# A decoder trunk in split fp32: column units split while token tile 1's first steps are issued

## The chip, the cores and the metric

The kernel runs on one core of one Trainium2 chip. The metric is the device time of one execution in microseconds (us), as the median of several runs; lower is better.

## The reference, cut to what matters

Two layers; each is a feed-forward sub-layer (FFN), a token-mixing sub-layer (Mix) and a second FFN, so six sub-layers one behind the other. All products are over 256 tokens and a model width of 1024.

```python
for l in range(DEPTH):                       # DEPTH = 2
    h = rms_norm(x, ffn1_pre_g[l])
    x = x + 0.5 * rms_norm(swiglu(h, ffn1_w1[l], ffn1_w2[l]), ffn1_post_g[l])
    h = rms_norm(x, mix_pre_g[l])
    z = h @ w_in[l]
    q, k, v, u_s, v_s, g_a, g_b = jnp.split(z, IN_SPLIT_POINTS, axis=-1)
    y_attn = sliding_window_attention(q, k, v, attn_sinks[l])
    y_sgu = spatial_gating(gelu(u_s), gelu(v_s), sgu_ln_g[l], sgu_ln_b[l], sgu_w[l], sgu_b[l])
    merged = (sigmoid(g_a) * (y_attn @ w_attn_branch[l])
              + sigmoid(g_b) * (y_sgu @ w_sgu_branch[l]))
    x = x + rms_norm(merged @ w_out[l], mix_post_g[l])
    h = rms_norm(x, ffn2_pre_g[l])
    x = x + 0.5 * rms_norm(swiglu(h, ffn2_w1[l], ffn2_w2[l]), ffn2_post_g[l])
```

## The kernel before, in words

**Split products.** Every fp32 operand is held as two parts, a high part (rounded) and a low part (what the rounding left), and a product is three matmuls: high by high, high by low, low by high (`passes`, and `feature_major` at L259 to L261, whose third matmul reads the low part of the weights).

**Weight units.** The weights come in units of 128x1024 floats (512 KB). `Stream` handles them in one fixed order. A unit is loaded by a DMA that SyncE issues (L119) into one of 4 `raw` buffers; ScalarE casts it to the high part (`wh`, L138); VectorE subtracts to get the low part (`wl`, L152, in `low`). Only then is the raw buffer free, so `low` of unit u issues the load of unit u + 4. The split pair goes into a ring of 9 places. `st.upto(n)` splits units in order up to n, and stops when the ring has no room (`free`); `st.done(u)` gives a place back. After the start, `slip` is set: the subtraction of a unit is issued behind the cast of the next, or where somebody calls `low`.

**Order.** The order of the instructions of every engine is the order in which the Python code calls them; nothing is moved by a scheduler, and each engine takes its own in that order.

**Between two sub-layers.** `project` multiplies the last product of a sub-layer, closes it (norm, residual, norm of the next one), and issues the next sub-layer's first product, whose rows are weight rows (`first`): token tile 0's `steps` first, then `finish(0, ...)`, then token tile 1's `steps`. A step is a few matmuls of one or half a unit. For tile 1 the first eight steps are `hi + lo` (four units of which are outside the ring), the others are `rest`. In `rest`, step 0 is preceded by `high` and `low` of tile 0 (L523 on ScalarE and L527 on VectorE: the input of the column products, scaled, in two parts), step `turn0` by a turn of tile 0's result, and behind every second step one unit of the column products is split (L597, L598). In Mix `turn0` is 2, and the turn is a transposition on TensorE (L380), a cast on ScalarE (L381), and on VectorE a chain of 16 instructions (L384 to L398) that normalises `vs`. A second such turn, that of tile 1, comes in `middle` ahead of column unit 4.

**Column products.** `middle` multiplies the column units. In Mix these are eight units u0 to u7 of `self.u`, then eight of `self.q`, and so on, each 24 matmuls of 256 columns (L259 to L261). Here u8 and on stand for the units behind u7, so u8 is the first of `self.q`. Behind unit j, `upto` splits as far as unit j + 7. Attention starts behind the fourteenth unit (L717, L718); it reads the queries that ScalarE and VectorE take out of PSUM (L841, L844). In an FFN the column units are taken by `feature_pair` (L272), 16 matmuls each.

Of the kernel before, what the change touches and what calls it, by code (L numbers as in the profile page):

```python
# [40 lines left out]
AHEAD = 7  # L41
# [22 lines left out]
def trunk(ctx: ExitStack, tc: tile.TileContext, a: dict, out: bass.AP):  # L64
# [100 lines left out]
    st = Stream()  # L165
# [237 lines left out]
    def project(units, lhs, k_post, gpost, gpre, nxt, xt, behind=None):  # L403
# [110 lines left out]
        first = nxt.first  # L514
# [4 lines left out]
        def quarter(t, h):  # L519
            return og[t].rearrange("p (a b) -> p a b", a=KD)[:, h * 4:h * 4 + 4, :]  # L520

        def high(t, h, ps):
            nc.scalar.copy(xth[:, h * 4:h * 4 + 4, rows_of(t)], ps)  # L523

        def low(t, h, ps):
            at = (slice(None), slice(h * 4, h * 4 + 4), rows_of(t))
            nc.vector.tensor_tensor(out=xtl[at], in0=ps, in1=f(xth[at]), op=ALU.subtract)  # L527
# [19 lines left out]
        hi, lo, rest = first.steps(0, xth, xtl)[:3]  # L547
# [36 lines left out]

        first.begin(1)
        hi, lo, rest = first.steps(1, xth, xtl)[:3]
        for s in hi + lo:
            s()
        for i, s in enumerate(rest):
            if i == 0:  # L590
                for h in range(2):
                    high(0, h, quarter(0, h))
                    low(0, h, quarter(0, h))
            if i == first.turn0:
                turn0()
            s()
            if i % 2:  # L597
                st.upto(min(st.ready + 1, first.units[-1] + 1 + AHEAD))  # L598
# [333 lines left out]
    first = subs[0].first  # L932
# [104 lines left out]
    for i, sub in enumerate(subs):  # L1037
        last = i == len(subs) - 1
        nxt = None if last else subs[i + 1]
        gains = []  # L1040

        def early():

            gains.append(gain(sub.post, i // 3))
            if not last:
                gains.append(gain(nxt.pre, (i + 1) // 3))
            if i == 0:
                nc.sync.dma_start(sinks, a["attn_sinks"].unsqueeze(0).partition_broadcast(P))
            if isinstance(nxt, Mix):
                nxt.tables()  # L1050

        behind = sub.middle(both, *xt, turn1, early)
        turn1 = project(sub.rows, sub.lhs, sub.k_post, gains[0], None if last else gains[1], nxt, xt, behind)
# [54 lines left out]
```

## Time and the profile before

| what | value |
|---|---|
| median of 3 runs | 1203.17 us (1202.26 to 1206.29) |
| the profiled execution: its time / its span | 1199.29 us / 1197.6 us |
| TensorE (PE) busy | 1176.7 us, 98% of the span |
| VectorE (DVE) / ScalarE (ACT) busy | 835.8 us (70%) / 677.9 us (57%) |
| mean granted TensorE clock | 0.996 |
| DMA | 220.90 MB, mean 184 GB/s |

The span runs from the first to the last instruction; the 1.7 us between it and the execution's own time lie around it. PE is the engine of the matmuls and PEld its weight loads; an engine's row names the source line, the operation, the tile it writes and the tile it reads. Idle time of an engine is put down to the instruction that ended it.

### The profile page before, as it was taken

Reading aid. Unit: us, or ns where it says so; the run is one execution under the profiler, and the core shown is the slowest. Engines: PE = TensorE matmul, PEld = TensorE weight load, DVE = VectorE, ACT = ScalarE, POOL = GpSimd, SP = SyncE. Lnnn points to the kernel's source line nnn. Section 1 sums busy time; section 2 is a strip of 40 time slices with the busy share of each in tenths; the row PEclk is TensorE's granted clock in tenths of the full one; section 3 lists DMA queues with packets and bytes.
Section 4 is the critical chain, followed back from the end, with each engine's and each line's share of the span. In section 5 each row is a group of like instructions: output and inputs, shape, how many; then the busy total and the mean of one; then the engine's idle time right before and its main releaser. Section 6 shows DMA issues by size and latency. Waiting matters only on the chain.

```text
span 1197.6 us, 18409 instructions
## 1 busy us (share of the span) xinstructions
PE 1176.7 (98%) x7031; PEld 1047.8 (87%) x7031; DVE 835.8 (70%) x1423; ACT 677.9 (57%) x1143; POOL 60.0 (5%) x40
## 2 busy tenths in 40 slices
PE   9999999999999999999999999999999999999997
PEld 7888888899999888888888888888999998888886
DVE  6767748678775976666576776577878768676653
ACT  5657544447676555655455665444567664665641
POOL 0000000001112100000000000000012040000000
PEclk9999999999999999999999999999999999999999
DMA  7577674465456637558626657735544664565660
GB/s 246 182 251 235 218 240 132 137 226 157 127 153 206 201 96 239 194 185 261 222 83 219 219 188 258 222 113 176 187 150 133 185 197 137 171 199 192 198 208 35
DMA packets 61288, 220.90 MB, mean 184 GB/s; under 512 B 7056, under 2 KB 7056, under 8 KB 61200
## 3 DMA queue, kind: packets, MB, share of 16 engines
q1 hardware_dynamic: 60912, 219.46, 56.3%
q8 instruction: 55, 0.90, 0.3%
q14 instruction: 33, 0.27, 0.1%
q10 hardware_dynamic: 288, 0.27, 0.1%
HBM read 218.65 MB, written 1.05 MB: 183 GB/s over the span
## 4 chain that ended last, share of the span: by engine, by line
PE 87%; DVE 6%; DMA 3%; ACT 1%; issue 1%; SPq 0%; DVEq 0%; ACTq 0%
PE mm L272 34%; PE mm L252 31%; PE mm L261 6%; PE mm L259 6%; PE mm L260 6%; DMA raw<-in_w_in 3%; DVE wl L152 2%; PE mm L217 1%; PE mm L754 1%; ACT wh L138 1%; DMA raw<-in_ffn_w 1%; PE mm L717 1%; PE mm L718 1%; PE mm L767 0%; PE mm L766 0%
## 5 line engine op out<-in xcount | busy, mean ns | idle before, releaser
L152 DVE TENSOR_TENSOR wl<-raw,wh 128x1024 fp32r<-128x1024 f32 x372 | 454.6, 1251 | 114.2 <-ACT wh L138 113.5
L138 ACT CAST wh<-raw 128x1024 fp32r<-128x1024 f32 x372 | 382.6, 1050 | 192.7 <-DMA raw<-in_ffn_w 75.1
L272 PE MATMUL mm<-xt,wh 128*128 128x512 f32 x1152 | 290.7, 393 | 0.7 <-DVE xt L948 0.7
L252 PE MATMUL mm<-wh,m 128*128 128x512 f32 x832 | 258.7, 390 | 0.0
L272 PEld LDWEIGHTS mm<-xt,wh 128*128 128x128 f32 x1152 | 207.6, 189 | 38.2 <-DVE xt L948 1.2
L252 PEld LDWEIGHTS mm<-wh,m 128*128 128x128 f32 x832 | 156.3, 188 | 32.0
L272 PEld LDWEIGHTS mm<-xt,wl 128*128 128x128 f32 x1152 | 157.2, 191 | 11.2
L252 PE MATMUL mm<-wl,m 128*128 128x512 f32 x416 | 162.1, 390 | 0.0
L272 PE MATMUL mm<-xt,wl 128*128 128x256 f32 x1152 | 160.7, 283 | 0.0
L261 PE MATMUL mm<-xt,wl 128*128 128x256 f32 x512 | 146.7, 287 | 5.0 <-DVE wl L152 5.0
L259 PE MATMUL mm<-xt,wh 128*128 128x256 f32 x512 | 147.7, 289 | 0.0
L260 PE MATMUL mm<-xt,wh 128*128 128x256 f32 x512 | 146.2, 285 | 0.0
L632 DVE TENSOR_TENSOR t<-mm,t 128x256 f32<-128x256 f32 x144 | 60.7, 422 | 96.8 <-ACT t L631 96.8
L261 PEld LDWEIGHTS mm<-xt,wl 128*128 128x128 f32 x512 | 99.5, 194 | 5.4 <-DVE wl L152 5.4
L260 PEld LDWEIGHTS mm<-xt,wh 128*128 128x128 f32 x512 | 99.6, 195 | 0.2
L259 PEld LDWEIGHTS mm<-xt,wh 128*128 128x128 f32 x512 | 99.6, 195 | 0.2
L252 PEld LDWEIGHTS mm<-wl,m 128*128 128x128 f32 x416 | 78.2, 188 | 15.9
L631 ACT COPY t<-mm 128x256 f32<-128x256 f32 x144 | 52.9, 367 | 46.5 <-PE mm L272 46.2
L634 ACT ACTIVATE t<-t 128x256 f32<-128x256 f32 x72 | 30.1, 418 | 75.9 <-DVE t L632 75.9
L259 PE MATMUL mm<-m,wh 128*128 128x256 f32 x256 | 72.7, 284 | 0.0
L260 PE MATMUL mm<-m,wh 128*128 128x256 f32 x256 | 72.5, 283 | 0.0
L261 PE MATMUL mm<-m,wl 128*128 128x256 f32 x256 | 72.5, 283 | 0.0
(156 smaller groups left out, 1327.3 us busy)
## 6 DMA issues: line engine op xcount, KB each, us to landing
raw<-in_ffn_w SPq DMA_DIRECT2D x264, 512.0 KB, 4.4
raw<-in_w_in SPq DMA_DIRECT2D x84, 512.0 KB, 4.4
raw<-in_w_sgu_branch SPq DMA_DIRECT2D x16, 512.0 KB, 3.7
raw<-in_w_attn_branch SPq DMA_DIRECT2D x16, 512.0 KB, 4.4
raw<-in_w_out SPq DMA_DIRECT2D x16, 512.0 KB, 4.6
gain<-in_ffn_post_g SPq DMA_DIRECT2D x4, 512.0 KB, 6.5
gain<-in_ffn_pre_g SPq DMA_DIRECT2D x3, 512.0 KB, 6.2
x<-in_x SPq DMA_DIRECT2D x4, 256.0 KB, 4.3
```

The source lines that it names most:

```text
L138: nc.scalar.copy(h, self.raw[u])
L152: nc.vector.tensor_tensor(out=lo, in0=self.raw.pop(u), in1=f(h), op=ALU.subtract)
L217: nc.tensor.transpose(ps[:, k, :], src[:, (c0 + k) * P:(c0 + k + 1) * P], ident)
L252: nc.tensor.matmul(o, every[i][0], every[i][1], start=start and i == 0, stop=stop and i == 2)
L259: nc.tensor.matmul(o, wh[:, ks], ah[:, k, :], start=(k == 0), stop=False)
L260: nc.tensor.matmul(o, wh[:, ks], al[:, k, :], start=False, stop=False)
L261: nc.tensor.matmul(o, wl[:, ks], ah[:, k, :], start=False, stop=(k == KD - 1))
L272: nc.tensor.matmul(out_, w[:, k * P:(k + 1) * P], x, start=(i == 0), stop=(i == len(todo) - 1))
L631: nc.scalar.copy(y[:, half, :], o[half][:, S:2 * S])
L632: nc.vector.tensor_tensor(out=y[:, half, :], in0=o[half][:, 0:S], in1=y[:, half, :], op=ALU.add)
L634: nc.scalar.activation(y[:, 0, :], y[:, 0, :], AF.Silu)
L717: nc.tensor.matmul(s[r][:, i, :], q_, kth[:, g, 0:nk], start=True, stop=False)
```

## The change

While token tile 1's eight first steps (`hi + lo`) are issued, one unit is split behind the first, third, fifth and seventh of them, if the ring has a place.

```diff
         first.begin(1)
         hi, lo, rest = first.steps(1, xth, xtl)[:3]
-        for s in hi + lo:
+        for i, s in enumerate(hi + lo):
             s()
+            if i % 2 == 0:
+                st.upto(min(st.ready + 1, first.units[-1] + 1 + AHEAD))
         for i, s in enumerate(rest):
             if i == 0:
                 for h in range(2):
```

`project` issues this between every two sub-layers, so five times. Of the ring's 9 places, 6 are held by the first units of a Mix at that point and 4 by those of an FFN, which leaves 3 and 5. The number of instructions of each kind stays as it was; only places in the queues change. In the rows below a tile's name ends in running numbers; raw_341_1820, raw_344_1826, raw_345_1829 and raw_403_2033 are the raw buffers of the units u0 to u3 of layer 0's Mix.

ScalarE, between FFN1 and Mix of layer 0, from the cast of tile 0's values (L373) on; before:

```order
L373 ACTIVATE vv_410_2105<-mm_404_2059,ry_398_2021 128x2x64
L523 CAST xt_74_352<-t4_348_1833 128x4x128 x2
L138 CAST wh_417_2160<-raw_341_1820 128x1024
L381 CAST kth_411_2106<-mm_419_2163 128x2x128
L138 CAST wh_431_2206<-raw_344_1826 128x1024
L138 CAST wh_435_2219<-raw_345_1829 128x1024
L138 CAST wh_438_2231<-raw_403_2033 128x1024
L138 CAST wh_441_2243<-raw_433_2210 128x1024
L138 CAST wh_444_2255<-raw_437_2223 128x1024
```

and now:

```order
L373 ACTIVATE vv_410_2105<-mm_404_2059,ry_398_2021 128x2x64
L138 CAST wh_417_2124<-raw_341_1820 128x1024
L138 CAST wh_419_2135<-raw_344_1826 128x1024
L138 CAST wh_422_2147<-raw_345_1829 128x1024
L523 CAST xt_74_352<-t4_348_1833 128x4x128 x2
L138 CAST wh_425_2175<-raw_403_2033 128x1024
L381 CAST kth_411_2106<-mm_428_2181 128x2x128
L138 CAST wh_440_2224<-raw_421_2139 128x1024
L138 CAST wh_444_2237<-raw_424_2151 128x1024
L138 CAST wh_447_2249<-raw_427_2179 128x1024
```

The casts of u0, u1 and u2 now stand ahead of the two L523, and four casts instead of one ahead of L381.

VectorE at the same place. Before, the subtractions of u0 to u4 stand behind the end of the turn's chain:

```order
L396 SCALAR_TENSOR_TENSOR n8_409_2104<-n8_409_2104,mv_421_2172,gain_412_2107 128x1024
L398 SCALAR_TENSOR_TENSOR n8_409_2104<-n8_409_2104,ry_430_2190,gain_413_2109 128x1024
L152 TENSOR_TENSOR wl_418_2161<-raw_341_1820,wh_417_2160 128x1024
L152 TENSOR_TENSOR wl_432_2207<-raw_344_1826,wh_431_2206 128x1024
L152 TENSOR_TENSOR wl_436_2220<-raw_345_1829,wh_435_2219 128x1024
L152 TENSOR_TENSOR wl_439_2232<-raw_403_2033,wh_438_2231 128x1024
L152 TENSOR_TENSOR wl_442_2244<-raw_433_2210,wh_441_2243 128x1024
```

Now three of them stand ahead of the chain's first instruction (L384):

```order
L374 SCALAR_TENSOR_TENSOR vv_410_2105<-mm_404_2059,ry_398_2021,vv_410_2105 128x2x64
L152 TENSOR_TENSOR wl_418_2125<-raw_341_1820,wh_417_2124 128x1024
L152 TENSOR_TENSOR wl_420_2136<-raw_344_1826,wh_419_2135 128x1024
L527 TENSOR_TENSOR xt_74_352<-t4_348_1833,xt_74_352 128x4x128 x2
L152 TENSOR_TENSOR wl_423_2148<-raw_345_1829,wh_422_2147 128x1024
L384 TENSOR_TENSOR ktl0_12_131<-mm_428_2181,kth_411_2106 64x2x128
L384 TENSOR_TENSOR ktl1_13_132<-mm_428_2181,kth_411_2106 64x2x128
```

Behind the chain's L398 the subtractions of u3, u4 and u5 follow, then L368 twice and L374, then that of u6. SyncE's list of loads keeps its order; the loads of u4, u5 and u6 follow the subtractions of u0, u1 and u2 and so go to an earlier place against the other engines.

VectorE between Mix and FFN2 of layer 0, before and now:

```order
L315 SCALAR_TENSOR_TENSOR t2_857_4639<-mm_814_4487,ry_847_4572,t2_856_4638 128x512
L527 TENSOR_TENSOR xt_74_352<-t4_797_4396,xt_74_352 128x4x128 x2
L152 TENSOR_TENSOR wl_861_4667<-raw_787_4352,wh_860_4666 128x1024
L152 TENSOR_TENSOR wl_863_4676<-raw_790_4371,wh_862_4675 128x1024
L152 TENSOR_TENSOR wl_866_4688<-raw_793_4389,wh_865_4687 128x1024
L152 TENSOR_TENSOR wl_869_4700<-raw_794_4392,wh_868_4699 128x1024
L170 TENSOR_TENSOR m8_855_4637<-mm_874_4717,m8_854_4636 128x4x128
```

```order
L315 SCALAR_TENSOR_TENSOR t2_857_4639<-mm_814_4487,ry_847_4572,t2_856_4638 128x512
L152 TENSOR_TENSOR wl_861_4647<-raw_787_4352,wh_860_4646 128x1024
L152 TENSOR_TENSOR wl_863_4654<-raw_790_4371,wh_862_4653 128x1024
L152 TENSOR_TENSOR wl_866_4663<-raw_793_4389,wh_865_4662 128x1024
L527 TENSOR_TENSOR xt_74_352<-t4_797_4396,xt_74_352 128x4x128 x2
L152 TENSOR_TENSOR wl_869_4671<-raw_794_4392,wh_868_4670 128x1024
L152 TENSOR_TENSOR wl_872_4688<-raw_864_4657,wh_871_4687 128x1024
L152 TENSOR_TENSOR wl_875_4706<-raw_867_4666,wh_874_4705 128x1024
L170 TENSOR_TENSOR m8_855_4637<-mm_880_4729,m8_854_4636 128x4x128
```

Three subtractions went ahead of L527, and on ScalarE four casts went ahead of L523 in the same way.

## Rows read from the trace of the kernel before

**Rows 1.** The page, busy time of each engine, its share of the span, and the number of its instructions.

```profile
PE 1176.7 (98%) x7031; PEld 1047.8 (87%) x7031; DVE 835.8 (70%) x1423; ACT 677.9 (57%) x1143; POOL 60.0 (5%) x40
```

**Rows 2.** The view of waits, TensorE alone: engine, tile and line that waited, what it waited for; us in total, times, longest.

```profile
PE mm L261 <- DVE wl L152: 5.0, 2, 2.5
PE mm L717 <- DVE m L844: 4.1, 4, 1.8
```

**Rows 3.** The timeline of TensorE at the start of the column products of layer 0's Mix: start, us, engine, line, operation, tiles; in brackets the idle time before it and who ended it. The last line is the transposition ahead of column unit 4.

```profile
225.34 0.28 PE L259 MATMUL mm<-xt,wh 128*128 128x256 f32 x1
...
228.28 0.58 PE L261 MATMUL mm<-xt,wl 128*128 128x256 f32 x1 [2.55 <-DVE wl L152]
...
229.09 0.42 PE L261 MATMUL mm<-xt,wl 128*128 128x256 f32 x1
...
229.73 0.41 PE L261 MATMUL mm<-xt,wl 128*128 128x256 f32 x1
...
231.60 0.28 PE L261 MATMUL mm<-xt,wl 128*128 128x256 f32 x1
...
231.96 0.28 PE L261 MATMUL mm<-xt,wl 128*128 128x256 f32 x1
...
241.08 0.38 PE L380 MATMUL mm<-ident,t 128*128 128x128 f32 x2
```

**Rows 4.** The same in layer 1's Mix.

```profile
815.94 0.28 PE L259 MATMUL mm<-xt,wh 128*128 128x256 f32 x1
...
818.80 0.58 PE L261 MATMUL mm<-xt,wl 128*128 128x256 f32 x1 [2.47 <-DVE wl L152]
...
831.60 0.38 PE L380 MATMUL mm<-ident,t 128*128 128x128 f32 x2
```

**Rows 5.** Stretches around the two waits: us, busy time of each engine with its instructions, then the granted clock (PEclk, 1.00 is 2.4 GHz, 0.50 is 1.2 GHz), the DMA engines' share and GB/s.

```profile
228.30:231.60 3.30, 3.30 (x15) 3.30 (x16) 3.30 (x3) 0.00 (x0) 0.00 (x0) 0.51 0.71 180
231.60:241.00 9.40, 9.40 (x81) 9.40 (x80) 6.48 (x9) 6.67 (x9) 0.00 (x0) 1.00 0.83 273
818.80:822.10 3.30, 3.29 (x15) 3.30 (x16) 3.30 (x3) 0.00 (x0) 0.00 (x0) 0.51 0.64 192
274.00:278.00 4.00, 1.79 (x15) 1.54 (x14) 3.91 (x6) 3.92 (x6) 0.00 (x0) 1.00 0.57 201
```

**Rows 6.** The timeline of VectorE around the first wait, then around the second turn's chain (L384 at 246.39) and on to the queries (L844).

```profile
213.31 1.29 DVE L527 TENSOR_TENSOR xt<-t,xt 128x512 fp32r<-128x512 f32 x2 [0.16 <-ACT xt L523]
220.38 0.86 DVE L384 TENSOR_TENSOR ktl<-mm,kth 64x256 fp32r<-64x256 f32 x2 [5.79 <-ACT kth L381]
...
227.01 4.63 DVE L152 TENSOR_TENSOR wl<-raw,wh 128x1024 fp32r<-128x1024 f32 x4
...
234.30 0.49 DVE L368 TENSOR_SCALAR t<-mm 128x128 f32<-128x128 f32 x2
236.27 0.29 DVE L374 SCALAR_TENSOR_TENSOR vv<-mm,vv 128x128 fp32r<-128x128 f32 x1 [1.48 <-ACT vv L373]
...
246.39 0.86 DVE L384 TENSOR_TENSOR ktl<-mm,kth 64x256 fp32r<-64x256 f32 x2 [2.02 <-ACT kth L381]
...
275.74 1.41 DVE L844 SCALAR_TENSOR_TENSOR m<-mm,m 64x512 fp32r<-64x512 f32 x2
```

**Rows 7.** The timeline of ScalarE over the same stretch. The cast at 213.69 is that of u0, the three at 220.18 those of u1 to u3, that at 231.96 is u4's, that at 245.04 u10's.

```profile
212.66 1.13 ACT L523 CAST xt<-t 128x512 fp32r<-128x512 f32 x2
213.69 1.05 ACT L138 CAST wh<-raw 128x1024 fp32r<-128x1024 f32 x1
219.91 0.37 ACT L381 CAST kth<-mm 128x256 fp32r<-128x256 f32 x1 [5.17 <-PE mm L380]
220.18 2.94 ACT L138 CAST wh<-raw 128x1024 fp32r<-128x1024 f32 x3
231.96 1.05 ACT L138 CAST wh<-raw 128x1024 fp32r<-128x1024 f32 x1 [8.84 <-DMA raw<-in_w_in]
...
245.04 1.05 ACT L138 CAST wh<-raw 128x1024 fp32r<-128x1024 f32 x1 [1.93 <-DMA raw<-in_w_in]
245.99 0.36 ACT L381 CAST kth<-mm 128x256 fp32r<-128x256 f32 x1
```

**Rows 8.** The timeline of SyncE's DMA queue, and the page's row on the loads of `w_in`: KB each, median us to landing.

```profile
228.29 26.32 SPq L119 DMA_DIRECT2D raw<-in_w_in  x11
...
raw<-in_w_in SPq DMA_DIRECT2D x84, 512.0 KB, 4.4
```

**Rows 9.** TensorE at the first attention matmuls, layer 0 and then layer 1, and VectorE in layer 1 at the start of the second turn's chain.

```profile
276.48 0.33 PE L717 MATMUL mm<-kth,m 128*128 128x128 f32 x1 [1.83 <-DVE m L844]
...
866.66 0.33 PE L717 MATMUL mm<-kth,m 128*128 128x128 f32 x1 [1.50 <-DVE m L844]
...
835.85 0.85 DVE L384 TENSOR_TENSOR ktl<-mm,kth 64x256 fp32r<-64x256 f32 x2 [1.17 <-ACT kth L381]
```

**Rows 10.** The passage from Mix to FFN2 of layer 0: ScalarE, VectorE, and TensorE's first column matmul.

```profile
429.41 1.13 ACT L523 CAST xt<-t 128x512 fp32r<-128x512 f32 x2
430.44 3.89 ACT L138 CAST wh<-raw 128x1024 fp32r<-128x1024 f32 x4
...
431.52 4.63 DVE L152 TENSOR_TENSOR wl<-raw,wh 128x1024 fp32r<-128x1024 f32 x4
...
438.81 1.77 PE L272 MATMUL mm<-xt,wh 128*128 128x512 f32 x7
```

## The prediction, made before the changed kernel was run

> **What bounds the kernel now.** I read the page first: TensorE is busy for 1176.7 us, 98% of the span [rows 1], so an edit that removes no matmul can gain only where TensorE stands still or runs slowly, and it can lose wherever it makes it stand still. Next the view of waits for TensorE alone: in the whole span two groups matter, 5.0 us in two waits of the column products' third matmul (L261) for a weight subtraction on VectorE, and 4.1 us in four waits of the first attention matmuls (L717) for the queries [rows 2]. Both lie in Mix; the three passages into an FFN have no wait in either group. Then the timelines of these places. In layer 0, TensorE begins unit u0 at 225.34, and stands from its second matmul until 228.28 for `wl` of u0 [rows 3]; in layer 1 the same happens from 815.94 to 818.80 [rows 4]. The unit is late because VectorE does the whole chain of tile 0's turn first, L384 at 220.38 to L398 before 227.01, and only then the subtraction [rows 6]. ScalarE cast u0 at 213.69, long before, so the unit's load and cast are not what is late [rows 7]. Last the granted clock in stretches: in the 3.3 us right behind each wait it is 0.51, the lower level of 1.2 GHz, and 1.00 again from 231.6 on [rows 5]. Three matmuls then take 0.64 us (229.09 to 229.73) instead of 0.36 (231.60 to 231.96) [rows 3].
>
> **What the two waits cost.** From the start of u0 to the transposition ahead of u4 lie four units of 24 matmuls. At 0.36 us for three, 96 matmuls take 11.52 us. Measured: 241.08 - 225.34 = 15.74 us in layer 0 [rows 3], so 4.22 us too many, and 831.60 - 815.94 = 15.66 us in layer 1 [rows 4], 4.14 too many. Of the 8.36 us, 5.0 are the idle time and 3.3 the slow clock behind it.
>
> **What moves in the passages into Mix.** The ring has three places, and the steps take them: the casts of u0, u1 and u2 go ahead of the two L523, their subtractions ahead of the chain. ScalarE is free for them at 212.66, when it now begins L523 [rows 7]. Their raw data has long landed: the casts of u1 to u3 run at 220.18 back to back with no wait [rows 7]. So three casts of 1.05 end at about 215.8, and the L523 pair (1.13) at 216.9 instead of 213.8. On VectorE the subtractions take 1.16 each (4.63 for four) [rows 6]: u0 and u1 from 213.8 to 216.1, then L527 (1.29) until about 217.6, then u2 until 218.8. L384 waits for ScalarE's L381, which waits for TensorE, and runs at 220.38 [rows 6]; so VectorE has 1.6 us to spare and the chain still ends at 227.0. Ahead of L381 ScalarE now has the cast of u3 too. It takes the ring place of a first unit that TensorE leaves one step (six matmuls) before its own transposition, so it ends about where L381 now starts at 219.91; up to 0.6 us later costs the chain 0.6 us and TensorE nothing, since u0, u1 and u2 (8.64 us of matmuls) are ready. L527's result is needed at 225.34, when the column products begin, 7.7 us behind it. At 225.34 TensorE finds u0 whole and goes on. u3 is needed at 225.34 + 8.64 = 233.98 and ready at 228.2. **Term 1: both waits and both slow stretches go, -8.36 us.** What hides the moved work are VectorE's 5.79 us and ScalarE's 5.17 us of idle time ahead of L384 and L381 [rows 6, 7]; without that cover each unit would put off the chain by 1.05 to 1.16 us.
>
> **The loads behind it.** The subtractions free raw buffers, so the loads of u4, u5 and u6 are issued at about 215, 216 and 219 instead of from 228.29 on [rows 8], in time in which the DMA has nothing to move. From 228.2 on the loads of u7, u8 and u9 take the places in time that u4, u5 and u6 had. So the stream stands three units further while TensorE is 4.2 us, one and a half units, earlier.
>
> **What is late next: the queries (L717).** The second turn's chain starts on VectorE at 246.39, when TensorE has left its transposition 5 us before (241.08): L381 stood behind u10's cast, which waited for its load until 245.04 [rows 3, 6, 7]. The subtractions and the queries (L844 at 275.74) come behind that chain, 29.35 us later, and TensorE waits for them until 276.48 and once more behind it [rows 6, 9]. Now u10's load follows u6's subtraction: 227.0, three subtractions (3.5), L368 and L374 (0.8), u6 (1.2), so 232.5; 4.4 us to landing [rows 8] gives 236.9, cast and L381 end at 238.4. TensorE's transposition is then at 241.08 - 4.22 = 236.9, so nothing else holds L384. It starts at 238.4, 8.0 us earlier, and 3.8 earlier against TensorE: more than the 2.2 us that layer 0 waits there. For layer 1 the same moment is 238.4 + 590.6 = 829.0 (815.94 - 225.34 = 590.6); the chain started at 835.85 [rows 9], so 6.8 earlier, 2.7 against TensorE, where 1.9 are waited. The trace shows no case in which the stretch from L384 to L844 runs with the loads in this other order, so I bound the term: from both sides all 4.1 us may go, or, if u10 takes twice the median to land (8.8 us), L384 starts at 242.8, 0.6 us later against TensorE than now, and each layer waits that much more, a loss of 1.2. The working lies near the upper end; since the stretch holds loads and ScalarE's casts that may stretch, I take three quarters. **Term 2: -3.1 us, bounds -4.1 and +1.2.**
>
> **What moves in the passages into an FFN.** There the ring has room for all four. ScalarE begins L523 at 429.41 and the four casts take 3.89 [rows 10]: L523 now starts at about 433.4. On VectorE L527 follows three subtractions and ends at about 435.7, then u3's ends at 436.9. TensorE begins the column products at 438.81 [rows 10]: 3.1 us to spare. The casts of u4 to u6 now stand ahead of tile 1's activation; their loads follow the earlier subtractions, and TensorE does not read what they delay until later units. **Term 3: 0.** Were that cover gone, every us would be paid three times, and the clock might fall as in Mix.
>
> **The rule of the queue.** ScalarE's rows show that the order of the program is kept even where a cast could run: u1's cast at 220.18 stands idle behind L381, which waits 5.17 us for TensorE [rows 7]. The Trainium skill (TensorE: Matmul & The Clock Gate, Part 1, the paragraph on engine queue depths) says that ScalarE's and VectorE's queues are strictly first in, first out; by that rule the casts now put ahead of L523 would hold it for as long as any of them waits, which is the slower rival below, and with no wait among them the sum stays as it is.
>
> **The sum.** 8.36 + 3.1 = 11.5 us. The profiled execution took 1199.29 us, so 1187.8 for one like it. The median of the runs is 3.9 us above it, so for a median I predict 1203.17 - 11.5 = **1191.7 us**. A difference of 0.3%, 3.6 us, is what a measurement of this kernel can tell from none.
>
> **The rivals.**
> - Only term 1 holds (chance 0.17): the queries keep their wait or add the 1.2 us. Gain 7.2 to 8.4: 1194.8 to 1196.0. For it: VectorE is saturated from the chain to the queries, and one late load delays all behind it. Against it: the 8 us worked out above.
> - The wait goes, but a slow clock comes elsewhere (0.07): the clock fell behind both waits of about 2.5 us and stayed at 1.00 with 1.83 us idle at L717 [rows 3 to 5, 9]. If such a wait remains and now draws a slow stretch, each costs what the old one did, 3.3 in all: gain 8.36 - 3.3 = 5.0: 1198.1. The same page of the Trainium skill says in Part 1 that the moment of a clock change is not tied to the program and that the count of slow matmuls differs between runs of one kernel; no run here shows that yet.
> - The wait moves to L717 whole (0.05): if L381 of the second turn still starts at 246, because u10 lands 8 us later than worked out, TensorE arrives 4.2 us earlier and waits 4.2 us longer in each layer, and the slow clock comes with it: gain 0, 1203.2.
> - Slower (0.04): one of the casts put ahead of L523 waits in the FFN passages. The point is 3.1 us of delay of L527. A cast that waits for one whole landing (4.4) leaves a wait of 1.3 us plus a slow stretch of 1.65, three times 2.95: 8.9 us, which eats term 1. Two landings, 8.8, leave 5.7 + 1.65, three times 7.35 = 22.1: 1191.7 + 22.1 = 1213.8. Against it: the four casts run back to back in 3.89 us [rows 10], so the data is there.
>
> That the ring leaves no room, so that nothing moves, is excluded by the instruction order.
>
> **How the numbers follow.** The forecast (gain 9.5 to 12.5, 1190.7 to 1193.7) has 0.67. Range: the first three cases reach from 1190.7 to 1198.1; below it I allow for runs that stand like the profiled one against the median, 1187. So 1187 to 1198, which leaves out about 1 in 10 by the cases. Faster by over 0.3%: 0.67 + 0.17 + 0.07 = 0.91, less a little for runs that scatter: 0.90. Within 0.3%: 0.06. Slower: 0.04.
>
> **What would show it.** Right: no wait of L261 for L152; 11.5 us from u0's start to the transposition ahead of u4 in both layers; granted clock 1.00 throughout both Mix; the second L384 6 to 8 us earlier; the waits at L717 under 1 us together; SyncE's loads of u4 to u6 issued before the chain. Wrong: any wait of L272 at the start of an FFN's column products, a wait of L717 over 2 us, or a late L381.

## The result and the profile after

The changed kernel takes 1185.7 us (median; 1185.57 to 1190.44) against 1202.98 us (1202.26 to 1206.29) for the kernel before: a ratio of 0.986, with a 95% interval of 0.985 to 0.988, or 17.3 us less. The prediction was 1191.7 us, 11.5 us less, with a range of 1187 to 1198. The direction was right, and the gain too small: the result lies 1.3 us below the range. Its own trace is that of its slowest run, 1190.44 us with a span of 1188.7.

TensorE's line of the page, and its view of waits (engine, tile and line that waited, what it waited for; us in total, times, longest), in that trace. Lines behind L587 are numbered two higher than before, so L719 is the old L717 and L846 the old L844.

```profile
PE 1173.2 (99%) x7031; PEld 1044.6 (88%) x7031; DVE 836.3 (70%) x1423; ACT 678.4 (57%) x1143; POOL 60.0 (5%) x40
...
PE mm L719 <- DVE m L846: 3.0, 2, 2.7
PE mm L252 <- ACT m L138: 2.4, 2, 2.0
PE mm L217 <- DVE t L449: 0.5, 1, 0.5
```

The 5.0 us of L261 behind L152, which led [rows 2], are gone. The attention matmuls still wait 3.0 us, all of it in layer 0; layer 1's 1.9 us are gone. A wait of L717 over 2 us was one of the prediction's signs of being wrong, and this run has one of 2.7; the second trace, below, has none.

TensorE from u0's first matmul to the transposition ahead of u4 in layer 0 and in layer 1, then the granted clock of the first of these stretches and of the 3.4 us behind the wait that is left in layer 0 (columns as in [rows 5]):

```profile
224.84 0.28 PE L259 MATMUL mm<-xt,wh 128*128 128x256 f32 x1
...
236.36 0.38 PE L380 MATMUL mm<-ident,t 128*128 128x128 f32 x2
...
813.69 0.28 PE L259 MATMUL mm<-xt,wh 128*128 128x256 f32 x1
...
825.22 0.38 PE L380 MATMUL mm<-ident,t 128*128 128x128 f32 x2
...
225.30:236.90 11.60, 11.60 (x99) 11.60 (x98) 10.27 (x11) 3.81 (x5) 0.00 (x0) 1.00 0.65 200
273.80:277.20 3.40, 3.40 (x17) 3.40 (x17) 3.37 (x10) 1.44 (x2) 0.00 (x0) 0.50 0.55 182
```

It takes 236.36 - 224.84 = 11.52 us, to the hundredth what the prediction made of 96 matmuls at full clock, where it was 15.74 [rows 3], and 825.22 - 813.69 = 11.53 us in layer 1. But in this run the wait at L719 drew a slow stretch.

VectorE and ScalarE over the same passage, to be laid beside [rows 6] and [rows 7], and SyncE's loads beside [rows 8]:

```profile
213.23 2.36 DVE L152 TENSOR_TENSOR wl<-raw,wh 128x1024 fp32r<-128x1024 f32 x2 [0.59 <-ACT wh L138]
215.65 1.30 DVE L527 TENSOR_TENSOR xt<-t,xt 128x512 fp32r<-128x512 f32 x2
216.86 1.22 DVE L152 TENSOR_TENSOR wl<-raw,wh 128x1024 fp32r<-128x1024 f32 x1
219.88 0.86 DVE L384 TENSOR_TENSOR ktl<-mm,kth 64x256 fp32r<-64x256 f32 x2 [1.81 <-ACT kth L381]
226.50 3.49 DVE L152 TENSOR_TENSOR wl<-raw,wh 128x1024 fp32r<-128x1024 f32 x3
...
238.90 1.05 ACT L138 CAST wh<-raw 128x1024 fp32r<-128x1024 f32 x1 [3.25 <-DMA raw<-in_w_in]
239.86 0.36 ACT L381 CAST kth<-mm 128x256 fp32r<-128x256 f32 x1
240.25 0.86 DVE L384 TENSOR_TENSOR ktl<-mm,kth 64x256 fp32r<-64x256 f32 x2 [3.35 <-ACT kth L381]
...
258.75 1.05 ACT L138 CAST wh<-raw 128x1024 fp32r<-128x1024 f32 x1 [5.37 <-DMA raw<-in_w_in]
259.82 1.23 DVE L152 TENSOR_TENSOR wl<-raw,wh 128x1024 fp32r<-128x1024 f32 x1 [4.24 <-ACT wh L138]
...
271.83 1.41 DVE L846 SCALAR_TENSOR_TENSOR m<-mm,m 64x512 fp32r<-64x512 f32 x2
...
214.48 33.99 SPq L119 DMA_DIRECT2D raw<-in_w_in  x11
```

Three subtractions stand ahead of the chain, which begins at 219.88 and ends before 226.50: half a us earlier than before, as TensorE's u0 is (224.84 and 225.34). The first of the released loads goes out at 214.48 instead of 228.29. The second chain starts at 240.25, 6.1 us earlier than before. The queries of layer 0 come late in this run behind a late load: the cast at 258.75 waited 5.37 us for it, and the subtraction at 259.82 waited 4.24 us for that cast.

### The profile page after: what moved, and what is told of

Read it like the earlier page. It is cut to its first block, busy times and chain, and to the rows that moved or that the text cites. A ratio compares the mean times of both kernels' runs of the same rounds, so it can differ in the third digit from the quotient of the medians.

```text
span 1188.7 us, 18407 instructions
## 1 busy us (share of the span) xinstructions
PE 1173.2 (99%) x7031; PEld 1044.6 (88%) x7031; DVE 836.3 (70%) x1423; ACT 678.4 (57%) x1143; POOL 60.0 (5%) x40
## 4 chain that ended last, share of the span: by engine, by line
PE 92%; DVE 3%; DMA 3%; ACT 1%; issue 1%; SPq 0%; DVEq 0%; ACTq 0%
PE mm L272 34%; PE mm L252 33%; PE mm L259 7%; PE mm L260 7%; PE mm L261 7%; DMA raw<-in_w_in 2%; PE mm L217 1%; PE mm L756 1%; DVE wl L152 1%; PE mm L720 1%; PE mm L719 1%; DMA raw<-in_ffn_w 1%; PE mm L769 0%; PE mm L768 0%; ACT wh L138 0%
## 5 line engine op out<-in xcount | busy, mean ns | idle before, releaser
L152 DVE TENSOR_TENSOR wl<-raw,wh 128x1024 fp32r<-128x1024 f32 x372 | 455.6, 1250 | 117.5 <-ACT wh L138 116.1
L261 PE MATMUL mm<-xt,wl 128*128 128x256 f32 x512 | 145.3, 284 | 0.0
L261 PEld LDWEIGHTS mm<-xt,wl 128*128 128x128 f32 x512 | 98.6, 193 | 0.0
L261 PE MATMUL mm<-m,wl 128*128 128x256 f32 x256 | 72.4, 283 | 0.0
```

Source lines behind the costliest of these rows:

```text
L152: nc.vector.tensor_tensor(out=lo, in0=self.raw.pop(u), in1=f(h), op=ALU.subtract)
L261: nc.tensor.matmul(o, wl[:, ks], ah[:, k, :], start=False, stop=(k == KD - 1))
```

## The experiments

The result left two questions. Why is the gain of the medians 17.3 us, when the two traces (1199.29 and 1190.44 us) are 8.9 us apart? And what freed the queries? Times below are medians; a ratio is to runs of the kernel before on the same chip, with its 95% interval.

### The kernel before, again

> The kernel before once more, for a second trace and for the spread of its runs. Theory A (the slow clock that the first trace did not show): the runs lie at 1202 to 1206 us, and in a trace at 1202 to 1203 us the two waits of L717 are as long as in the first one (about 2 us a layer) but each is followed by a slow stretch, so that four slow stretches stand in the two Mix instead of two: 1199.3 + 2 x 1.67 = 1202.6. Theory B (the loads): the clock falls only twice, behind the L261 waits, and the L717 waits are longer by 3 to 4 us together. Theory C (elsewhere): both are as in the first trace and the difference lies in another wait, at the start or between sub-layers.

1200.45 us, ratio 0.999 (0.996 to 1.001): a little quicker than theory A gave. Its runs go from 1198.29 to 1207.67 us, those of the comparison beside it from 1197.52 to 1207.93. Each execution has its mean granted clock on record, and over four such sets of runs of this same kernel (75 executions) time and clock go together:

```
mean clock      executions   median us   lowest to highest us
0.988 to 0.989       6        1207.8     1204.6 to 1208.1
0.990 to 0.991      19        1205.1     1202.6 to 1207.2
0.992 to 0.993      31        1202.2     1200.3 to 1205.8
0.994 to 0.995       9        1199.5     1198.2 to 1200.9
0.996 to 0.997       9        1198.5     1197.3 to 1201.0
```

The 75th had 0.998 and took 1197.13 us. (One with a recorded clock of 0.94 at a usual time, 1205.05 us, is left out.) A straight line through all 75 falls by 1.2 us for every 0.001 of clock, and 0.001 of 1200 us is 1.2 us: so the spread of 10 us is for the most part slow clock. The new trace (1200.88 us) shows where it lies. Waits, then three stretches at the lower clock, behind L261 in layer 0, behind L717 in layer 0, and behind L261 in layer 1:

```profile
PE mm L261 <- DVE wl L152: 5.0, 2, 2.5
PE mm L717 <- DVE m L844: 3.6, 4, 1.6
...
230.20:233.60 3.40, 3.40 (x19) 3.40 (x18) 1.92 (x3) 1.04 (x1) 0.00 (x0) 0.50 0.91 294
278.00:281.40 3.40, 3.40 (x18) 3.40 (x18) 3.37 (x10) 1.37 (x2) 0.00 (x0) 0.50 0.47 172
820.70:824.10 3.40, 3.32 (x15) 3.33 (x16) 3.40 (x4) 0.00 (x0) 0.00 (x0) 0.50 0.68 183
```

The waits are no longer than in the first trace [rows 2]; a wait of 1.64 us at L717 has drawn a slow stretch, where 1.83 us had drawn none [rows 5, 9]. Theories B and C fall; A holds in kind, though this run had one such stretch and not two. (The trace of the run with only the passages into an FFN, below, has both.)

### The changed kernel, again

> The changed kernel once more, for a second trace. Theories A and B alike: most runs at 1185.6 to 1186.2 us with no wait over 0.5 us at the attention matmuls in either layer and no slow stretch inside either Mix; the first trace's 1190.4 us is the run in which a late load kept layer 0's wait (2.66 + 0.38 us) and its slow stretch (1.67 us), 4.7 us in all. Theory C: the trace still has that wait and is faster somewhere else.

1186.65 us, ratio 0.987 (0.984 to 0.989). The new trace is of a run at 1186.33 us; the two stretches cover both Mix from u0 to past the attention's start:

```profile
PE mm L719 <- DVE m L846: 0.4, 1, 0.4
...
225.30:285.00 59.70, 59.56 (x501) 59.45 (x501) 50.02 (x89) 32.18 (x54) 1.90 (x1) 1.00 0.59 195
810.00:870.00 60.00, 59.62 (x500) 59.49 (x500) 49.98 (x91) 32.83 (x57) 1.90 (x1) 1.00 0.58 194
```

Of the 9.1 and 8.6 us that TensorE waited at these two places in the two traces of before, 0.4 are left, and the clock is 1.00 throughout. As expected, the first trace is the exception: of 11 executions of the changed kernel nine lie between 1185.3 and 1187.3 us.

### Only the passages into a Mix, only those into an FFN

```diff
-            if i % 2 == 0:
+            if i % 2 == 0 and isinstance(nxt, Mix):        # the other run: not isinstance(nxt, Mix)
```

> The units are split behind the first steps only in the two passages into a Mix. My theory, that the whole gain is there: 1185.7 us, ratio to the kernel before 0.986, same as the changed kernel within 1 us. Rival, that the passages into an FFN give the part of the gain that I did not forecast (about 6 us): 1191 to 1192 us, ratio 0.990.

1185.68 us, ratio 0.986 (0.983 to 0.989).

> The units are split behind the first steps only in the three passages into an FFN. My theory: no change, 1203.0 us, ratio 1.000 within 0.002. Rival, that these passages give about 6 us: 1197 us, ratio 0.995.

1201.77 us, ratio 1.000 (0.997 to 1.002). The whole gain is in the two passages into a Mix; the other three give and cost nothing that can be told.

This trace also shows what no trace of the kernel before does. It is of a run at 1205.09 us, above the median, with the passages into Mix as they were before. Its waits (L719 is the old L717), then four stretches, behind L261 and behind L719 in layer 0 and the same in layer 1:

```profile
PE mm L261 <- DVE wl L152: 5.0, 2, 2.5
PE mm L719 <- DVE m L846: 4.0, 3, 2.2
...
228.30:231.70 3.40, 3.40 (x17) 3.40 (x17) 3.15 (x3) 0.00 (x0) 0.00 (x0) 0.50 0.73 218
276.10:282.90 6.80, 6.66 (x30) 6.50 (x31) 6.64 (x23) 3.24 (x6) 0.00 (x0) 0.50 0.71 210
822.30:825.60 3.30, 3.30 (x18) 3.30 (x17) 1.97 (x3) 1.05 (x1) 0.00 (x0) 0.50 0.98 302
870.10:876.80 6.70, 6.52 (x30) 6.55 (x31) 6.52 (x24) 3.17 (x8) 0.00 (x0) 0.50 0.65 226
```

The waits are those of [rows 2], 9.0 us for 9.1, but all four places now draw slow clock, 20.2 us of it, and behind the attention's waits the stretches are twice as long.

### The attention later, in the kernel before

```diff
-ATTEND = (27, 32, 38, 44, 50, 56)
+ATTEND = (29, 34, 38, 44, 50, 56)
```

> The kernel before with the first two attention calls one column unit (2.88 us of matmuls) later, so that the queries are there when TensorE comes to them; the wait of L261 for the first unit stays. Theory A (the spread of the kernel before comes from slow clock drawn by the L717 waits, on top of those behind L261): no wait of L717 over 0.5 us, the runs close up to within about 4 us, the median goes from 1203 to about 1195 to 1196 us (4.1 us of idle time and 3.5 us of slow clock less), ratio 0.993 to 0.994. Theory D (the spread comes from the L261 waits alone, which draw one or two slow stretches each from run to run): the median falls only by the idle time, to about 1199, and the spread of 10 us stays.

Ratio 0.995 (0.993 to 0.997). One of the nine executions took 4139.01 us, for which no run shows a cause; the other eight go from 1191.86 to 1198.69 us, and their median is 1195.28 us (1196.12 with the ninth). The trace is that of the quickest: L717 is down to 0.8 us, L261 waits as ever, and this time no slow clock follows it.

```profile
PE mm L261 <- DVE wl L152: 5.0, 2, 2.5
PE mm L717 <- DVE m L844: 0.8, 2, 0.4
...
227.76 0.39 PE L261 MATMUL mm<-xt,wl 128*128 128x256 f32 x1 [2.54 <-DVE wl L152]
...
228.00:232.00 4.00, 4.00 (x35) 4.00 (x35) 3.12 (x3) 0.65 (x1) 0.00 (x0) 1.00 0.73 224
```

The fall of 7.6 us (from 1202.89) is more than the 3.3 us of waiting that went, so the L717 waits did cost slow clock (A). But a spread of 6.8 us stays, and the same wait of 2.5 us at L261, which drew a slow stretch in every trace above, draws none in this one, which D says. So both waits contribute; that the slower executions of this run have their slow clock at L261 is not shown, since none of them was traced.

### One unit, two units

```diff
-            if i % 2 == 0:
+            if i == 0:                                     # the other run: if i in (0, 2):
```

> Only the first unit (u0) is split behind the first step, not four. Theory E: the L261 wait of 2.5 us goes in both layers (u1 is ready at 228.2, just when TensorE needs it), but only one load runs ahead, so u10's load is late by two units and the L717 waits stay at 2 to 4 us a layer with a slow stretch in many runs: 1191 to 1196 us, ratio 0.990 to 0.994. Rival F: 1185.7 to 1187 us, one unit is enough.

1198.86 us, ratio 0.997 (0.995 to 0.998), above what either theory gave. The waits, the queries' second chain, and the clock behind the queries:

```profile
PE mm L719 <- DVE m L846: 7.4, 3, 4.5
...
242.25 0.86 DVE L384 TENSOR_TENSOR ktl<-mm,kth 64x256 fp32r<-64x256 f32 x2 [0.62 <-ACT kth L381]
...
273.40:279.80 6.40, 6.40 (x31) 6.40 (x31) 6.25 (x23) 2.87 (x9) 0.00 (x0) 0.50 0.61 227
```

L261 waits no more, and TensorE is 4 us earlier; but it then waits 7.4 us for the queries instead of 4.1, and the slow stretch behind that is twice as long as the old ones. Of the 5.0 us of waiting that went at L261, 3.3 have come back here. That is in large part the rival to which I had given 0.05; a gain of 4.0 us is left.

> Two units (u0 and u1) are split behind the first steps. One unit gave 1198.9 us with L717 waits of 7.4 us, all of them 1185.7. Theory E (each load that runs ahead starts the second chain earlier by the time of one unit on the way from load to cast, about 2 us): L717 waits of 2 to 4 us in all, with a slow stretch in some runs: 1189 to 1194 us. Rival F': the step is not gradual, two units are like three, 1185.7 to 1187 us.

1196.46 us, ratio 0.994 (0.992 to 0.997), executions from 1191.86 to 1200.30; L719 waits 4.7 us in the trace, 4.0 of them in layer 0. So it is gradual from one unit to two, but slower than I expected, and the changed kernel, with a third unit split ahead of the chain and a fourth cast ahead of L381, is 10.8 us quicker still.

### The loads held back

In the first attempt the loads of u4 to u6 are only issued later in the program.

```diff
-                self.load(u + 1 + RAW)
+                if not self.hold:
+                    self.load(u + 1 + RAW)
...
+        st.hold = isinstance(nxt, Mix)
         for i, s in enumerate(hi + lo):
...
             if i == first.turn0:
                 turn0()
+            if i == first.turn0 + 1:
+                st.hold = False
```

> The changed kernel, but in the passages into a Mix the loads that the early subtractions would issue (u4 to u6) are held back until the subtraction of u3, behind the chain of the turn, where the kernel before had them. Theory E (the L717 waits went because the loads run ahead): term 1 stays, no wait of L261, but u10's load comes as late as before while TensorE is 4.2 us earlier, so the waits of L717 are 5 to 6 us in each layer, with a slow stretch each: 1185.7 + 11 + 3.4 = about 1200 us, ratio 0.997. Rival F (they went because the subtractions no longer stand behind the chain, whatever the loads do): 1185.7 to 1187 us, ratio 0.986.

1186.36 us, ratio 0.987 (0.985 to 0.989): like the changed kernel. But this says nothing against E, since the loads were not held. The first of them goes out at 214.52, as without the edit (214.48):

```profile
214.52 32.71 SPq L120 DMA_DIRECT2D raw<-in_w_in  x11
```

SyncE has nothing else in its list there, and starts each load when its raw buffer is free, wherever the code calls it. So the hold was tied to the chain by a load that has to wait for it, in the next run:

```diff
+            if i == first.turn0 + 1 and isinstance(nxt, Mix):
+                lnb = nxt.into[5]
+                nc.sync.dma_start(lnb[:, 0:8], a["sgu_ln_b"][nxt.l:nxt.l + 1, 0:8].partition_broadcast(P))
+                st.hold = False
```

> As the run with the loads held back, but so that they are really late: in the list of SyncE a small load (8 columns of the second gain, the same values) stands ahead of them, which has to wait until the turn's chain has read that gain, so u4 to u6 are loaded from about 227 us on. The subtractions stay early. Theory E (the loads that run ahead are what frees the queries): u10's load comes two units later than in the changed kernel, its second chain starts 2.5 to 4 us later, and each layer waits 2 to 4 us at L717 with a slow stretch in most runs: 1190 to 1196 us, ratio 0.990 to 0.995. Rival F (what counts is that the subtractions stand ahead of the chain): 1185.7 to 1187.5 us, ratio 0.986.

1200.24 us, ratio 0.997 (0.996 to 0.999), in twelve executions from 1198.7 to 1201.0. SyncE's queue, the waits, and the clock behind them:

```profile
226.97 0.33 SPq L603 DMA_DIRECT2D gain<-in_sgu_ln_b  x1
227.39 24.45 SPq L120 DMA_DIRECT2D raw<-in_w_in  x11
...
PE mm L726 <- DVE m L853: 8.3, 2, 5.0
...
273.56 0.47 PE L726 MATMUL mm<-kth,m 128*128 128x128 f32 x1 [3.30 <-DVE m L853]
273.50:280.00 6.50, 6.32 (x28) 6.16 (x29) 6.30 (x24) 2.94 (x4) 0.00 (x0) 0.50 0.62 209
```

The subtractions are as early as in the changed kernel (the first at 213.58, there at 213.23), TensorE no longer waits at L261, and yet 14.5 us of the gain are gone: with the loads at 227.39 TensorE waits 8.3 us for the queries, and a slow stretch of double length comes with that in each layer. This is E, at a higher price than expected. Early subtractions without early loads only move the wait.

### The gains later

```diff
-            at((5, 1), early)
+            at((16, 1), early)
```

> The changed kernel with Mix's two gain vectors (512 KB each) loaded behind the sixteenth column unit instead of the sixth, so that they no longer stand ahead of u15's load on SyncE. Theory G (what is left of the L717 wait is u15's load behind the gains, as in the first trace of the changed kernel): no wait of L717 in either layer in any run, the spread shrinks, median 1184.5 to 1185.5 us, ratio to before 0.985. Rival: the gains are hidden already, 1185.7 us, and runs at 1187 to 1190 us still occur.

1185.64 us, ratio 0.987 (0.984 to 0.989), five executions from 1185.40 to 1187.35, and no wait of L719 in the trace. Two of 11 executions of the changed kernel lie above 1189 us and none of these five, which is too few to tell. Whether the gains' loads caused the wait of the first trace stays open.

## Why the prediction was right and wrong, point by point

**Term 1 (-8.36 us).** Right in the trace: 11.52 us from u0 to the transposition ahead of u4, no wait of L261, the chain not put off. It was worked from an execution in which each wait drew one slow stretch; the traced execution of the kernel with the later attention drew none there.

**Term 2 (-3.1 us).** Right in mechanism, a little small. In the second trace the waits of L717 fall from 4.1 to 0.4 us, so 3.7, near the bound. The second chain was to start at 238.4; it started at 239.3 to 240.3. That the loads carry this term was argued in the prediction and is shown by the held loads. What the term left out is the clock: it priced the L717 waits at their idle time alone, since the one wait that the prediction looked at left the clock at 1.00 [rows 5].

**Term 3 (0).** Right: the FFN passages alone give 1.000. L527 ends at 432.8 in the first of them, and TensorE begins the column products at 436.45: 3.6 us to spare, where 3.1 were worked out.

```profile
431.53 1.29 DVE L527 TENSOR_TENSOR xt<-t,xt 128x512 fp32r<-128x512 f32 x2
...
436.45 1.77 PE L272 MATMUL mm<-xt,wh 128*128 128x512 f32 x7
```

**The sum.** This is the step that failed. It gave 1187.8 us "for one like" the profiled execution, and for that it was right within 1.5 us: the second trace of the changed kernel is of a run at 1186.33. Then it said that the median of the runs "is 3.9 us above it" and took the same 11.5 us from that median, as if what sets the median apart would stay. But those 3.9 us were more of what the change removes. The trace of before, with a mean clock of 0.996, stood at the quick end of the runs: executions near the median of the comparison, 1202.98 us, have about 0.992 by the table, and (0.996 - 0.992) x 1200 = 4.8 us more slow clock. The run at 1205.09 us shows it behind the same waits: 20.2 us at the lower clock, so 10.1 us lost, where the prediction found 3.3. Against the second trace of the changed kernel (1186.33 us) its idle time of 9.0 - 0.4 = 8.6 us and these 10.1 make 18.7 of the 18.8 us between the two. In medians: idle time in Mix 9.1 - 0.4 = 8.7 us; clock from 0.992 to 0.998, 0.006 x 1200 = 7.2 us; together 15.9 of 17.3 us. The last 1.4 us are open: the clock is given to 0.001, which is 1.2 us, and the idle times are those of single traces.

**The rivals.** I had the clock that changes from run to run among them, as a way in which the gain could be smaller; it was true, and of the kernel before. The Trainium skill (TensorE: Matmul & The Clock Gate, Part 1) says, of the start of a kernel, that the count of slow matmuls differs between runs of one kernel; the 75 executions agree, with clocks from 0.989 to 0.998, and the traces show the slow stretches in the middle of it. The wait that moves whole to L717 was a good rival too: one unit shows it in large part (7.4 of 9.1 us of waiting stay), and without the early loads the changed kernel would nearly have been it (8.3 us, 1200.24 us). The slower case did not occur.

## What to carry to other kernels

Where the median of the runs stands off the profiled execution, ask first what differs, by the clock of each run: a wait that draws a slow clock in some runs costs more in the median than in a trace that happened to be quick. Removing a wait of the bounding engine pays only as far as the next supplier is early by the same amount; here the loads that went out with the early subtractions did that, and without them 14.5 of 17 us would have been lost at the next wait. A load on a queue that has nothing else to issue starts when its buffer is free (here at 214.52 us with the later call, 214.48 without); calling it later in the code alone holds nothing back.

## What the runs showed of the hardware

- A wait of the same length may or may not lower TensorE's clock: 2.54 us left it at 1.00 in one execution, and about 2.5 us was followed by 0.50 in others; 1.83 us at the first attention matmul left it, 1.64 us did not. Nor did the length of the wait set how long the lower level lasted: 3.4 us behind waits of 2.66 and 0.38 us at the attention in the first trace of the changed kernel, 6.4 us and more behind 2.58 and 0.38 us with one unit, and 6.8 us behind 1.50 us with only the FFN passages edited.
- So the kernel before spreads over 10 us on one chip with identical work. The changed kernel, whose TensorE waits 3.0 us and 0.4 us for the queries in its two traces and no longer for u0, spreads over 5 us, nine of 11 executions within 2 us.
